# All 31 taps of the first block's depthwise convolution as matmuls with diagonal matrices read from memory

## The chip, the cores and the metric

The kernel runs on 1 core of one Trainium2 chip, in one launch. The metric is device time in microseconds (us) of that core; the figure for a kernel is the median of its runs. Before the change it is 2170.08 us, the median of 3 runs from 2164.84 to 2173.29 us.

## The reference

The program is a network of two blocks over 256 tokens of width 1024. The first block has two layers (`DEPTH = 2`), and each of them has a mixer with three branches: a gated delta rule, a convolution branch and a softmax attention with a forgetting gate ("fox"). What the change touches is the convolution branch:

```python
CONV_WIDTH = D_MODEL // 4      # 256 channels
CONV_KERNEL = 31

def causal_depthwise_conv(x, w):
    k_width, channels = w.shape
    return lax.conv_general_dilated(
        x, w[:, None, :], window_strides=(1,), padding=[(k_width - 1, 0)],
        dimension_numbers=('NWC', 'WIO', 'NWC'), feature_group_count=channels)

# in hybrid_mixer, once a layer
glu_a, glu_b = jnp.split(c_glu, 2, axis=-1)
u = glu_a * jax.nn.sigmoid(glu_b)
u = causal_depthwise_conv(u, cnv_dw_w) + cnv_dw_b
o_b = jax.nn.silu(layer_norm(u, cnv_ln_g, cnv_ln_b))
...
mixed = jnp.concatenate([o_a, o_b, o_c], axis=-1) * mix_scale
return jnp.einsum('bte,ed->btd', mixed, w_out)
```

Each channel has its own 31 taps; output t of a channel is the sum over j of `w[j] * u[t - 30 + j]`. All values are float32.

## The kernel before, in words

The stages follow one another: first block, layer 0 (mixer, dense feed-forward), layer 1 (mixer, mixture of experts), then the second block. `mixer1` is called once a layer, with l = 0 and l = 1. Its matrix products are split in three: a float32 weight tile that has landed in `raw` is rounded on ScalarE to `wh` (line 172), the remainder `wl` is made on VectorE (line 174), and three single-pass matmuls (lines 183 to 185) take the place of one float32 product. A product of two plain float32 operands is recorded as two MATMUL instructions, here called two passes.

Weights come by `load` (line 166): one DMA of up to 1 MB issued by SyncE into one of four `raw` buffers, in rotation. A load waits until the four-before-it buffer is free, that is until its `wh` and `wl` have been made.

Inside `mixer1` the generators `inverse`, `scan`, `fox`, `conv` and `gates` are emitted one after another. A scheduler then orders each engine's instructions by a simulated timeline in which what was emitted earlier goes first when it is ready. So the matmuls of `conv` and, behind them, of `gates` (`proj_b`, 48 matmuls) are put where the delta rule's inverse and scan and the attention leave TensorE free. Each engine then works through its list strictly in that order.

`conv` (lines 739 to 785) works on tiles with the 128 channels of a half on the partitions and 256 tokens along the free dimension. `cup` holds the gated input behind 30 zeros, so tap j of half c reads `up[:, c, j:j + T]`. The last taps of each half (6 in layer 0, 8 in layer 1) are matmuls: ScalarE scales the identity by the tap's column into `dgt` (line 756, two buffers), and a float32 matmul adds into the PSUM tile `a_conv` (recorded at line 362, the helper `mm`). The other taps (25 or 23 a half) are a chain on VectorE into `ccv`: line 762 for the first, line 764 for the rest. Line 765 adds the two parts. What follows in `conv` is the layer norm over channels with two sums on TensorE (`f_cmean`, `f_cvar`), the sigmoid, and the product.

At the end of the mixer the convolution's two halves become chunks 3 and 4 of the transposed operand `xT` (lines 802 and 803), the attention's chunks 5 to 7 and the delta rule's, behind the gates, 0 to 2 (`split_t`, lines 267, 277, 278). Then four `proj_b` products with `w_out` follow, each of which goes through the chunks in the order 0 to 7.

The names in the rows: `a_pB` is a `proj_b` product, `f_fl` are the attention's logits, `g_S`, `g_o` and `g_ws` belong to the scan, `g_lb`, `g_x` and `g_u` to the inverse. Instructions from `mm` all carry line 362.

Of the kernel before, what the change touches and what calls it, by code (L numbers as in the profile page):

```python
# [9 lines left out]
F32 = mybir.dt.float32  # L10
# [4 lines left out]
AF = mybir.ActivationFunctionType  # L15
ALU = mybir.AluOpType
# [4 lines left out]
P = 128  # L21
D = 1024
KC = D // P
T = 256
# [12 lines left out]
def make_consts():  # L37
    i = np.arange(P)
    r, c = i[:, None], i[None, :]
    same = (r // 64) == (c // 64)  # L40
    out = {}
    out["ident"] = (r == c)
    out["anti"] = (r + c == P - 1)
    out["tri"] = (r <= c)
    out["tri64"] = (r <= c) & same
    out["one64"] = same
    out["strict"] = (r < c)
    out["mcaus"] = np.where(c <= r, 0.0, NEG)
    out["iota"] = np.broadcast_to(c, (P, P))
    out["one16"] = (r // 16) == (c // 16)  # L50
    out["id64"] = (r % 64 == c[:, :64])
    out["mcaus64"] = np.where(r % 64 <= c[:, :64], 0.0, NEG)
    out["mstrict64"] = np.where(r % 64 < c[:, :64], 0.0, NEG)
    out["low32"] = (r % 32 == c[:, :32]) | ((r % 32 >= 16) & (c[:, :32] < 16))
    out["id16"] = (r % 16 == c[:, :16])
    out["in16"] = (r // 16 % 4 == c[:, :4])
    out["even16"] = (r // 16 % 2 == c[:, :2])
    out["even32"] = (r // 32 % 2 == c[:, :2])
    return np.ascontiguousarray(np.concatenate([np.asarray(out[n]).astype(np.float32) for n, _ in CONSTS], 1))
# [22 lines left out]

PCOLS1 = []
for _l in range(2):
    PCOLS1 += [(f"rowp{_l}", 24), (f"cw{_l}", 36), (f"mix{_l}", 8), (f"gnw{_l}", 1), (f"dww{_l}", 62), (f"dwb{_l}", 2),
               (f"clg{_l}", 2), (f"clb{_l}", 2)]
PCOLS1 += [("mix0g", 8), ("mix0b", 8)]
PCOLS2 = [("f1n", 8), ("mxn", 8), ("f2n", 8), ("men", 8), ("aqg", 1), ("akg", 1), ("mqg", 1), ("mkg", 1),
# [15 lines left out]
class Net:  # L104
# [249 lines left out]
    def mixer1(self, l, x, xT):  # L354
        nc, A, ident = self.nc, self.A, self.ident
        V, S, PE = nc.vector, nc.scalar, nc.tensor
        wA, wB, wS = A["w_in_a"], A["w_in_b"], A["w_in_s"]
        mp = self.mp
        half = (slice(0, 64), slice(64, 128))

        def mm(out, lhsT, rhs, start=True, stop=True, **kw):
            PE.matmul(out, lhsT, rhs, start=bool(start), stop=bool(stop), skip_group_check=True, **kw)


        rowp = self.col1(f"rowp{l}")
# [53 lines left out]
        cw = self.col1(f"cw{l}")  # L419
# [192 lines left out]
        def spare(c):  # L612

            names = TILES_A[2 * c:2 * c + 2]
            ps = self.proj_a(wA[l, c][:, :1024 * len(names)], xT, tiles=len(names))
            for i, n in enumerate(names):
                if n[0] == "v":
                    value(ps[:, i, :], int(n[1]))
                else:
                    S.activation({"b": glu[:, 0:2], "a": glu[:, 2:4], "f": foxqk[:, 0:3], "g": foxqk[:, 3:6]}[n[0]][:, int(n[1]), :],  # L620
                                 ps[:, i, :], AF.Copy)
# [116 lines left out]
        cv, csq = mp.tile([P, 2, T], F32, name="ccv"), glu[:, 0:2, :]  # L738

        def conv():  # L740

            for c in GLUC:
                spare(c)
            sg = glu[:, 0:2, :]
            self.sigmoid(sg, sg)
            up = mp.tile([P, 2, 30 + T], F32, name="cup")
            V.memset(up[:, :, 0:30], 0.0)
            V.tensor_tensor(up[:, :, 30:], glu[:, 2:4, :], sg, op=ALU.mult)
            yield
            near = 31 - (6, 8)[l]  # L750
            dw, db = self.col1(f"dww{l}"), self.col1(f"dwb{l}")
            pc = self.ps("a", "conv").rearrange("p (c n) -> p c n", c=2)
            for c in range(2):
                for j in range(near, 31):
                    dg = mp.tile([P, P], F32, name="dgt", bufs=2)
                    S.activation(dg, ident, AF.Copy, scale=dw[:, c * 31 + j:c * 31 + j + 1])
                    mm(pc[:, c, :], dg, up[:, c, j:j + T], start=j == near, stop=j == 30)
            for c in range(2):
                for j in range(near):
                    w = dw[:, c * 31 + j:c * 31 + j + 1]  # L760
                    if j == 0:
                        V.tensor_scalar(cv[:, c, :], up[:, c, 0:T], w, db[:, c:c + 1], op0=ALU.mult, op1=ALU.add)
                    else:
                        V.scalar_tensor_tensor(cv[:, c, :], up[:, c, j:j + T], w, cv[:, c, :], op0=ALU.mult, op1=ALU.add)
            V.tensor_tensor(cv, cv, pc, op=ALU.add)
            yield
            ps = self.ps("f", "cmean")
            for c in range(2):
                mm(ps[:, :T], self.ones, cv[:, c, :], start=c == 0, stop=c == 1)
            for c in range(2):  # L770
                V.scalar_tensor_tensor(cv[:, c, :], ps[:, :T], -1.0 / 256, cv[:, c, :], op0=ALU.mult, op1=ALU.add)
            S.activation(csq, cv, AF.Square)
            ps = self.ps("f", "cvar")
            for c in range(2):
                mm(ps[:, :T], self.ones, csq[:, c, :], start=c == 0, stop=c == 1)
            crs = glu[:, 2, :]
            self.rsqrt(crs, ps[:, :T], 1.0 / 256, 1e-5)
            lg_, lb_ = self.col1(f"clg{l}"), self.col1(f"clb{l}")
            for c in range(2):
                V.tensor_tensor(cv[:, c, :], cv[:, c, :], crs, op=ALU.mult)  # L780
                V.tensor_scalar(cv[:, c, :], cv[:, c, :], lg_[:, c:c + 1], lb_[:, c:c + 1], op0=ALU.mult, op1=ALU.add)
            V.tensor_scalar(csq, cv, -40.0, None, op0=ALU.max)
            self.sigmoid(csq, csq)
            V.tensor_tensor(cv, cv, csq, op=ALU.mult)
            yield
# [14 lines left out]
        for c in range(2):  # L800
# [3 lines left out]
                                   op0=ALU.mult, op1=ALU.subtract)  # L804
# [949 lines left out]
def pack_b(w, cols=256):  # L1754

    s, n, c = w.shape[:-2], len(w.shape) - 2, w.shape[-1]
    k = w.shape[-2] // P
    w = w.reshape(s + (k, P, c // cols, cols))
    w = w.transpose(tuple(range(n)) + (n + 2, n + 1, n, n + 3))
    return np.ascontiguousarray(w).reshape(s + (c // cols, P, k * cols))  # L1760
# [10 lines left out]
def chan(v, n):  # L1771

    return v.reshape(n, P).T
# [8 lines left out]
def zeros(*s):  # L1782
    return np.zeros(s, np.float32)


def pack_first(I):
    out = {"consts": make_consts()}
    w = I["w_in"]
    a = np.concatenate([w[:, :, W_IN_A], zeros(2, D, 128)], 2)
    out["w_in_a"] = pack_a(a)  # L1790
    out["w_in_b"] = pack_b(w[:, :, W_IN_B])
    out["w_in_s"] = pack_b(w[:, :, W_IN_S], 18)[:, 0]
    out["w_out"] = pack_b(I["w_out"])
    cols = {}
    for l in range(2):
        cw = I["gdn_conv_w"][l]
        cw = np.concatenate([cw[:, 384:768], cw[:, 0:384], cw[:, 768:]], 1)
        rowp = np.concatenate([I["gdn_dt_bias"][l], zeros(6), I["fox_f_bias"][l], I["gdn_a_log"][l]])
        cols[f"rowp{l}"] = np.broadcast_to(rowp, (P, 24))
        cols[f"cw{l}"] = cw.reshape(4, 9, P).transpose(2, 1, 0).reshape(P, 36)  # L1800
        cols[f"mix{l}"] = chan(I["mix_scale"][l], 8)
        cols[f"gnw{l}"] = np.concatenate([I["gdn_norm_w"][l]] * 2)[:, None]
        cols[f"dww{l}"] = I["cnv_dw_w"][l].reshape(31, 2, P).transpose(2, 1, 0).reshape(P, 62)
        cols[f"dwb{l}"] = chan(I["cnv_dw_b"][l], 2)
        cols[f"clg{l}"] = chan(I["cnv_ln_g"][l], 2)
        cols[f"clb{l}"] = chan(I["cnv_ln_b"][l], 2)
    cols["mix0g"], cols["mix0b"] = chan(I["ln_mix_g"][0], 8), chan(I["ln_mix_b"][0], 8)
    out["pcol1"] = np.ascontiguousarray(np.concatenate([cols[n] for n, _ in PCOLS1], 1))
    out["ln_mix"] = np.concatenate([np.stack([I["ln_mix_g"][l], I["ln_mix_b"][l]]) for l in range(2)])
    out["ln_ffn"] = np.concatenate([np.stack([I["ln_ffn_g"][l], I["ln_ffn_b"][l]]) for l in range(2)])  # L1810
    out["ffn_w1"] = pack_a(I["ffn_w1"][0])
    out["ffn_w3"] = pack_a(I["ffn_w3"][0])
    out["ffn_w2"] = pack_rows(I["ffn_w2"][0])
    out["router"] = pack_b(I["moe_router"][0], NE)[0]
    for n in ("moe_w1", "moe_w3"):
        w = I[n][0].reshape(NE, 2, 4, P, 7, 512).transpose(0, 4, 1, 3, 2, 5)
        out[n] = np.ascontiguousarray(w).reshape(NE, 7, 2, P, 2048)
    out["moe_w2"] = pack_rows(I["moe_w2"][0])
    return out
# [94 lines left out]
```

## Time and profile before

| | |
|---|---|
| time, median of 3 runs | 2170.08 us |
| the profiled execution's own time | 2177.81 us |
| its span | 2176.0 us |
| TensorE (PE) busy | 2079.3 us, 96% |
| VectorE (DVE) busy | 1295.8 us, 60% |
| ScalarE (ACT) busy | 1017.1 us, 47% |
| mixer of layer 0, its end (output projection) | about 181 us into the span |
| mixer of layer 1, its end (output projection) | about 586 us into the span |
| read from memory | 536.72 MB |

Times inside the span are counted from its start. PEclk is the TensorE clock that was granted, as a share of full speed: 1.00 is 2.4 GHz and 0.50 is 1.2 GHz. A matmul's recorded duration holds its latency in the pipeline, so the distance from one start to the next is what an instruction costs in a run of them; "busy" counts overlapping durations once. An engine works through its instructions in order, so what stands behind a waiting instruction waits too.

### The profile page before, as it was taken

The page shows a single profiled execution, that of the slowest core. Times are in us where ns is not written, and L with a number is a line of the kernel's source. Part 1 is how long each engine was busy: PE and PEld are TensorE (multiplying, and loading weights), DVE is VectorE, ACT ScalarE, POOL GpSimd, SP SyncE. Part 2 cuts the span into 40 slices and gives each one's busy share as a digit, 9 for nine tenths or more (in the row PEclk, how much of TensorE's full clock was granted, in tenths as well). Part 3 has the DMA queues.
Part 4 walks back from the last instruction along what each step waited for, and adds up shares of the span by engine and source line. Part 5 has one row for each costly group of instructions (what it writes and reads, how often), then busy time and mean ns, then how long its engine had stood idle before and what let it go on. Part 6 is the DMA issues. An engine that isn't in the chain of part 4 may idle for free. (4 is left out here: it accounts for less than half of the span.)

```text
span 2176.0 us, 31850 instructions
## 1 busy us (share of the span) xinstructions
PE 2079.3 (96%) x12770; PEld 1598.7 (73%) x12770; DVE 1295.8 (60%) x1903; ACT 1017.1 (47%) x1445; POOL 12.7 (1%) x27
## 2 busy tenths in 40 slices
PE   8998999899979999999999999999899999999998
PEld 7887999778766565565565565555699988888997
DVE  6767955676666555454564465454555568765444
ACT  6545444464435454444454454443444444644443
POOL 0000000000000000000000000000000000000000
PEclk9979999998889999999999999999999999999999
DMA  6313675422359999999999999999455553444552
GB/s 236 104 44 118 213 258 182 137 90 96 139 178 347 364 406 378 415 415 371 401 372 383 400 389 393 421 417 398 168 192 180 190 183 126 136 164 155 186 183 98
DMA packets 78987, 545.36 MB, mean 251 GB/s; under 512 B 8960, under 2 KB 11272, under 8 KB 13936
## 3 DMA queue, kind: packets, MB, share of 16 engines
q1 hardware_dynamic: 76112, 527.40, 63.8%
q0 software_dynamic: 2720, 15.84, 2.0%
q8 instruction: 103, 1.69, 0.3%
q14 instruction: 52, 0.43, 0.1%
HBM read 536.72 MB, written 6.49 MB: 250 GB/s over the span
## 5 line engine op out<-in xcount | busy, mean ns | idle before, releaser
L174 DVE TENSOR_TENSOR wl<-raw,wh 128x1024 fp32r<-128x1024 f32 (+1 forms) x662 | 798.1, 1217 | 432.3 <-ACT wh L172 420.5
L172 ACT ACTIVATE wh<-raw 128x1024 fp32r<-128x1024 f32 (+1 forms) x662 | 690.7, 1054 | 627.9 <-PE a_pA L184 270.3
L183 PE MATMUL a_pA<-xTh,wh 128*128 128x256 f32 x1456 | 419.0, 289 | 6.2 <-ACT foxqk L620 3.5
L185 PE MATMUL a_pA<-xTh,wl 128*128 128x256 f32 x1456 | 415.5, 286 | 0.8 <-DVE wl L174 0.7
L184 PE MATMUL a_pA<-xTl,wh 128*128 128x256 f32 x1456 | 415.6, 286 | 0.4 <-DVE xTl L278 0.2
L183 PEld LDWEIGHTS a_pA<-xTh,wh 128*128 128x128 f32 x1456 | 280.8, 193 | 14.7 <-ACT foxqk L620 5.6
L184 PEld LDWEIGHTS a_pA<-xTl,wh 128*128 128x128 f32 x1456 | 281.0, 193 | 5.3 <-issue 3.2
L185 PEld LDWEIGHTS a_pA<-xTh,wl 128*128 128x128 f32 x1456 | 280.8, 193 | 3.8 <-issue 2.2
L1033 PE MATMUL a_up<-raw,xef 128*64 128x512 f32 x896 | 213.5, 596 | 0.0
L184 PE MATMUL a_up<-wl,xeh 128*128 128x512 f32 x448 | 180.7, 403 | 0.5 <-DVE wl L174 0.4
L183 PE MATMUL a_up<-wh,xeh 128*128 128x512 f32 x448 | 177.7, 400 | 0.0
L185 PE MATMUL a_up<-wh,xel 128*128 128x512 f32 x448 | 177.3, 396 | 0.0
L1033 PEld LDWEIGHTS a_up<-raw,xef 128*64 128x64 f32 x896 | 65.1, 137 | 127.8 <-issue 122.3
L1038 DVE TENSOR_TENSOR mos<-mos,a_up 128x512 f32<-128x512 f32 x42 | 28.8, 685 | 200.3 <-PE a_up L1033 149.8
L183 PE MATMUL a_pB<-wh,xTh 128*128 128x256 f32 x480 | 141.5, 296 | 5.7 <-ACT glu L620 3.2
L185 PE MATMUL a_pB<-wh,xTl 128*128 128x256 f32 x480 | 138.6, 291 | 1.6 <-DVE xTl L278 1.6
L184 PE MATMUL a_pB<-wl,xTh 128*128 128x256 f32 x480 | 139.8, 292 | 0.0
L1066 PE MATMUL y_y<-raw,mof 128*64 128x512 f32 x448 | 132.8, 602 | 0.7 <-ACT mof L1052 0.7
L184 PEld LDWEIGHTS a_up<-wl,xeh 128*128 128x128 f32 x448 | 84.6, 189 | 34.5 <-issue 11.4
L183 PEld LDWEIGHTS a_up<-wh,xeh 128*128 128x128 f32 x448 | 84.7, 189 | 28.1 <-ACT wh L172 7.3
L185 PE MATMUL acc_acc<-wh,ffl 128*128 128x512 f32 x264 | 102.0, 392 | 0.0
L184 PE MATMUL acc_acc<-wl,ffh 128*128 128x512 f32 x264 | 101.9, 392 | 0.0
(556 smaller groups left out, 2703.2 us busy)
## 6 DMA issues: line engine op xcount, KB each, us to landing
raw<-in_moe_w_dram SPq DMA_DIRECT2D x336, 1024.0 KB, 9.2
raw<-in_ffn_in_dram SPq DMA_DIRECT2D x44, 1024.0 KB, 4.9
raw<-in_ffn_w_dram SPq DMA_DIRECT2D x33, 1024.0 KB, 5.0
raw<-in_w_in_a_dram SPq DMA_DIRECT2D x24, 1024.0 KB, 4.9
raw<-in_ffn_out_dram SPq DMA_DIRECT2D x22, 1024.0 KB, 4.9
raw<-in_w_out_dram SPq DMA_DIRECT2D x12, 1024.0 KB, 4.9
raw<-in_w_in_g_dram SPq DMA_DIRECT2D x12, 1024.0 KB, 4.9
raw<-in_w_in_b_dram SPq DMA_DIRECT2D x6, 1024.0 KB, 5.1
```

The source lines that it names most:

```text
L172: nc.scalar.activation(wh[:, :m], raw[:, o:o + m], AF.Copy)
L174: nc.vector.tensor_tensor(wl[:, :m], raw[:, o:o + m], wh[:, :m].bitcast(F32), op=ALU.subtract)
L183: mm(out, lh, rh, start=start, stop=False, skip_group_check=True)
L184: mm(out, lh, rl, start=False, stop=False, skip_group_check=True)
L185: mm(out, ll, rh, start=False, stop=stop, skip_group_check=True)
L1033: PE.matmul(ps[r], xe[0][:, k0, r], w[:, k * 512:k * 512 + 512], start=k0 == 0, stop=k0 == 7, skip_group_check=True)
L1038: V.tensor_tensor(s, s, pp[1], op=ALU.mult)
L1066: PE.matmul(py[h][r], hf[:, k, r], w[:, j * 1024 + h * 512:j * 1024 + h * 512 + 512], start=b == 0 and k == 0, stop=b == 6 and k == 3, ski ...
```

## The change

In both mixers all 62 products of a half and a tap become float32 matmuls. The diagonal matrices are no longer made on ScalarE: the host lays them out as an input `w_tap` (2 layers, 4 pieces, 128 x 2048; 1 MB a piece, 16 matrices a piece, 14 in the last), and `conv` reads the four pieces with `load`, by SyncE into the `raw` buffers, and uses them as they land, without `wh` and `wl`. The VectorE chain and the addition of the two parts are gone; instead two ACTIVATE instructions bring the PSUM tile to `ccv` and add the bias. The loads stand, in order of emission, between those for the gated input and the one for the gates.

```diff
-    PCOLS1 += [(f"rowp{_l}", 24), (f"cw{_l}", 36), (f"mix{_l}", 8), (f"gnw{_l}", 1), (f"dww{_l}", 62), (f"dwb{_l}", 2),
+    PCOLS1 += [(f"rowp{_l}", 24), (f"cw{_l}", 36), (f"mix{_l}", 8), (f"gnw{_l}", 1), (f"dwb{_l}", 2),
...
-            near = 31 - (6, 8)[l]
-            dw, db = self.col1(f"dww{l}"), self.col1(f"dwb{l}")
+            db = self.col1(f"dwb{l}")
             pc = self.ps("a", "conv").rearrange("p (c n) -> p c n", c=2)
+            for i in range(4):
+                raw = self.load(A["w_tap"][l, i]).rearrange("p (j n) -> p j n", n=P)
+                for n in range(16 * i, min(16 * i + 16, 62)):
+                    c, j = n // 31, n % 31
+                    mm(pc[:, c, :], raw[:, n % 16, :], up[:, c, j:j + T], start=n == 0, stop=n == 61)
             for c in range(2):
-                for j in range(near, 31):
-                    dg = mp.tile([P, P], F32, name="dgt", bufs=2)
-                    S.activation(dg, ident, AF.Copy, scale=dw[:, c * 31 + j:c * 31 + j + 1])
-                    mm(pc[:, c, :], dg, up[:, c, j:j + T], start=j == near, stop=j == 30)
-            for c in range(2):
-                for j in range(near):
-                    w = dw[:, c * 31 + j:c * 31 + j + 1]
-                    if j == 0:
-                        V.tensor_scalar(cv[:, c, :], up[:, c, 0:T], w, db[:, c:c + 1], op0=ALU.mult, op1=ALU.add)
-                    else:
-                        V.scalar_tensor_tensor(cv[:, c, :], up[:, c, j:j + T], w, cv[:, c, :], op0=ALU.mult, op1=ALU.add)
-            V.tensor_tensor(cv, cv, pc, op=ALU.add)
+                S.activation(cv[:, c, :], pc[:, c, :], AF.Identity, bias=db[:, c:c + 1])
...
+    taps = zeros(2, 64, P, P)
+    i = np.arange(P)
+    taps[:, :62, i, i] = I["cnv_dw_w"].reshape(2, 31, 2, P).transpose(0, 2, 1, 3).reshape(2, 62, P)
+    out["w_tap"] = np.ascontiguousarray(taps.reshape(2, 4, 16, P, P).transpose(0, 1, 3, 2, 4)).reshape(2, 4, P, 2048)
...
-        cols[f"dww{l}"] = I["cnv_dw_w"][l].reshape(31, 2, P).transpose(2, 1, 0).reshape(P, 62)
```

## Rows read from the trace of the kernel before

**Rows 1.** The page: busy time of each engine; granted clock in 40 slices.
```profile
PE 2079.3 (96%) x12770; PEld 1598.7 (73%) x12770; DVE 1295.8 (60%) x1903; ACT 1017.1 (47%) x1445; POOL 12.7 (1%) x27
...
PEclk9979999998889999999999999999999999999999
```
**Rows 2.** Windows, stretches of both mixers: length, busy per engine (instructions), clock, DMA.
```profile
core 0: us, PE busy (x) PEld busy (x) DVE busy (x) ACT busy (x) POOL busy (x), PEclk, DMA share, GB/s
...
122.20:146.10 23.90, 23.90 (x191) 16.58 (x187) 12.90 (x38) 8.85 (x32) 0.00 (x0) 0.50 0.01 2
146.10:165.80 19.70, 18.84 (x185) 16.94 (x183) 16.50 (x38) 9.15 (x18) 0.00 (x0) 1.00 0.16 54
165.80:181.00 15.20, 10.82 (x64) 8.85 (x65) 11.48 (x26) 9.70 (x23) 2.06 (x4) 0.86 0.31 118
...
525.00:552.30 27.30, 27.30 (x210) 19.18 (x210) 14.01 (x41) 10.36 (x36) 0.00 (x0) 0.50 0.00 1
552.30:573.10 20.80, 20.80 (x191) 18.36 (x190) 15.38 (x33) 9.99 (x19) 0.00 (x0) 1.00 0.02 4
573.10:586.00 12.90, 8.03 (x52) 5.86 (x51) 9.52 (x23) 8.92 (x21) 0.53 (x1) 1.00 0.96 384
```
**Rows 3.** Timeline of VectorE in mixer 0, an idle time in the half-clock stretch.
```profile
129.31 0.69 DVE L661 TENSOR_REDUCE fsx<-f_fl 128x2 f32<-128x512 f32 x1 [4.07 <-PE f_fl L362]
```
**Rows 4.** Timeline of TensorE, the mixers' ends, with the idle time before.
```profile
165.83 1.13 PE L362 MATMUL f_cmean<-ccv,ones 128*128 128x256 f32 x4 [0.81 <-DVE ccv L765]
...
174.49 0.66 PE L267 MATMUL g_tr<-call,mixed 128*128 128x128 f32 x4 [1.39 <-DVE mixed L816]
175.88 0.39 PE L183 MATMUL a_pB<-wh,xTh 128*128 128x256 f32 x1 [0.73 <-ACT xTh L277]
...
585.98 0.38 PE L183 MATMUL a_pB<-wh,xTh 128*128 128x256 f32 x1 [1.35 <-ACT xTh L802]
```
**Rows 5.** Tile ccv: the chain on VectorE and the addition of its end.
```profile
L764 DVE SCALAR_TENSOR_TENSOR ccv<-cup,p,ccv x92: 443/477/486, 122.6 to 565.4; 128x256 f32<-128x256 f32 x92
...
L765 DVE TENSOR_TENSOR ccv<-ccv,a_conv x2: 673/681/689, 165.1 to 571.7; 128x512 f32<-128x512 f32 x2
```
**Rows 6.** Tile dgt: duration in ns, min/median/max, first and last start, forms.
```profile
L362 PE MATMUL a_conv<-cup,dgt x56: 377/483/795, 123.0 to 571.3; 128*128 128x256 f32 x56
L756 ACT ACTIVATE dgt<-call,p x28: 385/401/404, 17.5 to 569.6; 128x128 f32<-128x128 f32 x28
```
**Rows 7.** Timeline of TensorE in mixer 0: start us, us, instruction, count.
```profile
77.67 1.88 PE L362 MATMUL g_lb<-sg,call 128*128 128x512 f32 x4
...
123.01 2.08 PE L362 MATMUL a_conv<-cup,dgt 128*128 128x256 f32 x4
125.02 0.79 PE L362 MATMUL f_fl<-rowsT,unit_m 18*128 18x256 f32 x2
...
156.74 1.08 PE L362 MATMUL a_conv<-cup,dgt 128*128 128x256 f32 x4
157.75 0.56 PE L362 MATMUL g_S<-late,kd 64*64 64x64 f32 x12
```
**Rows 8.** Groups by line and form: busy us, mean ns of one, idle before.
```profile
L362 PE MATMUL g_lb<-sg,call 128*128 128x512 f32 x24 | 11.8, 591 | 0.0
```
**Rows 9.** Windows of tile dgt alone: length, PE, PEld, ACT, clock, DMA.
```profile
122.20:146.10 23.90, 6.59 (x12) 3.35 (x12) 2.32 (x6) 0.50 0.01 2
```
**Rows 10.** Windows of tile a_pB alone: length, PE, PEld, DVE, ACT, clock, DMA.
```profile
146.10:165.80 19.70, 6.32 (x42) 5.49 (x42) 0.00 (x0) 0.60 (x1) 1.00 0.16 54
```
**Rows 11.** Timeline of SyncE's issues in mixer 0; DMA issue of one weight, KB, us to landing.
```profile
85.13 0.33 SPq L166 DMA_DIRECT2D raw<-in_w_in_b_dram  x1
93.27 19.83 SPq L166 DMA_DIRECT2D raw<-in_w_out_dram  x4
156.09 73.92 SPq L166 DMA_DIRECT2D raw<-in_ffn_w_dram  x8
...
raw<-in_w_out_dram SPq DMA_DIRECT2D x12, 1024.0 KB, 4.9
```

## The prediction

> **What bounds the kernel now.** I read the page first, for the engine that fills the span: TensorE is busy for 96% of it, and the row of the granted clock, at 9 (full) nearly everywhere, dips to 8 in slices that hold the mixers of layer 0 and layer 1 [rows 1]. Then I cut the stretches of both mixers in which the convolution runs into windows, by the granted clock [rows 2]. The reader is to see three stages in each. First a stage of 23.90 us (27.30 us in layer 1) in which TensorE is busy throughout and yet has half its clock, 0.50. Then one of 19.70 us (20.80 us) at full clock with TensorE busy for 18.84 us (all 20.80 us). Last a tail of 15.20 us (12.90 us) in which TensorE is busy for only 10.82 us (8.03 us), because the layer norm of the convolution, the gates and the transposes hand work to and fro.
>
> So up to the tail TensorE sets the pace. The timeline of VectorE bears it out from the other side: that engine, which carries the chain of taps, sits idle for 4.07 us before an instruction that waits for the attention's logits [rows 3], with taps queued behind it. The chain of taps shows on the path in one place only: TensorE waits 0.81 us for the addition at its end in mixer 0 [rows 4]. In the tail the waits are for the gated delta rule's result (1.39 us), for its transposes (0.73 us), and in layer 1 for the convolution's chunk of the output projection (1.35 us) [rows 4].
>
> **What the change removes.** On VectorE 92 chain instructions at 0.477 us and the four first ones, of another form, counted alike: 46 us in both mixers; and two additions of 0.68 us [rows 5]. On ScalarE 28 scaled identities at 0.40 us, 11 us [rows 6]. Both engines have free time in every stage (VectorE is busy for 12.90 of 23.90 and 16.50 of 19.70 us) [rows 2], so of this only what lies in the tail counts: the wait of 0.81 us, and little else. I book it with the tail below.
>
> **What it adds on TensorE.** Before, 56 passes in all [rows 6], which are 24 in mixer 0 (6 taps of 2 halves, 2 passes each) and 32 in mixer 1. After, 62 matmuls a mixer, 124 passes each: 100 more in mixer 0, 92 more in mixer 1, 192 in all. The price of one at full clock lies between two rows. A run of four passes took 1.01 us from its start to the start of the next group, 0.25 us each, with the first weight load not hidden [rows 7]. A longer stream is cheaper: four float32 passes of 512 columns took 1.88 us [rows 7], one of them has a recorded duration of 0.591 us [rows 8], so three distances fill the other 1.29 us, 0.43 us each; half of that, 0.215 us, for 256 columns. The new passes need nothing but `cup` and a landed piece, so they come in long runs, and I take 0.215 us: 192 x 0.215 = 41.3 us. At 0.25 us it would be 48 us. At half clock four passes took 2.01 us, 0.50 us each in a short run [rows 7]; in a long one it would be twice 0.215, 0.43 us.
>
> **Where these passes go.** In order of emission they stand behind the inverse, the scan and the attention, and ahead of the gates. So they take the gaps that those leave. In the half-clock stage the gaps are small: 12 of the 24 passes were run there in mixer 0, 6.59 of 23.90 us [rows 9], and the rest of the stage belongs to the attention's logits, on 18 rows of the array in the row shown [rows 7], and the inverse. A few gate matmuls in these gaps are replaced by passes. I take ten more passes there in both mixers together, at 0.215 us extra each: 2 us; between 0 and 20 us, if up to half of the added passes fell there. All others pile up after it. The full-clock stage was full already; there 42 gate matmuls, 6.32 us, were part of the filling [rows 10], and now they come after the convolution's. The stage grows by what is added, nearly one for one.
>
> **The tail.** Here something comes back. The gates' projection, about 6 us of dense work, now comes behind the convolution's last pass, and so covers part of the convolution's layer norm. The idle time of TensorE in the two tails is 15.20 - 10.82 = 4.4 us and 12.90 - 8.03 = 4.9 us [rows 2]. I take both back, 9.3 us; the other bound is nothing, as the gates' own sigmoid and products then come last and leave a tail of their own.
>
> **The clock.** In the half-clock stages TensorE was busy without a pause, and the clock stayed at 0.50 (1.2 GHz) for 23.90 and 27.30 us [rows 2]. The Trainium skill (TensorE: Matmul & The Clock Gate, "Why this matters for your kernels") says to keep TensorE busy continuously to get past the gate to the full clock. By that rule these stages should have been at full clock, and the trace disagrees. So I don't count on added busy time alone to lift it. For a lift speaks that the added passes use all 128 rows; against it, how few of them find room before 146 us. In the forecast both stages stay at half clock.
>
> **Loads, copies and the constants.** Four loads of 1 MB a mixer are added on SyncE's queue, ahead of the gates' load and the four of `w_out`. Those went out at 85.13 us and between 93.27 and about 113 us [rows 11]. These are the moments when buffers come free, and the first four now belong to the pieces. A load of this size lands in 4.9 us [rows 11], so the pieces are there by about 118 us, before the first pass at 123.01 us [rows 7]: nothing lost. The DMA engines are nearly idle then (share 0.01) [rows 2]. What is behind them moves late: the gates' load waits for the 16 matmuls of the first piece, the first three of `w_out` for the other pieces, the fourth for the gates' split. The third of them waits for the convolution's last pass; but it is needed only after the gates, the tail and two output products, so I cost it at nothing. With that cover gone it costs a landing and a split, an estimated 4.9 + 2 us a mixer. The next stage's first load, at 156.09 us before [rows 11], slips too; the output projection hides it. The bias is added by four ACTIVATEs of two halves of 256 columns, nearest to the scaled identity of 128 columns at 0.40 us [rows 6], in place of the two additions of 0.68 us [rows 5]: between 0 and 1 us lost, I take nothing. The table of constants loses 124 of its 290 columns; it is loaded behind others at the start, where the kernel waits for the inputs: nothing, at most 1 us gained.
>
> **Sum.** 41.3 + 2 - 9.3 = 34 us. The profiled execution took 2177.81 us around its span of 2176.0, 7.7 us more than the median of the runs, 2170.08; the difference carries over, so I add it to the median: 2204 us.
>
> **Rivals.**
> 1. *The clock comes back.* The place is the half-clock stages. If the full-row passes come in long unbroken runs early in them, they run at 2.4 GHz and give back up to half their length, 12.0 + 13.7 = 25.6 us. Then 34 - 2 - 25.6 = +6 us: 2176, no change that can be measured; if each stage recovers only in its middle, about +20, 2190. It decides from whether such runs stand before 130 us. For it: a pass is 128 rows deep. Against it: the convolution had half its passes in that stage before, and the clock did not rise. If, beyond that, VectorE's freed queue shortens the chains of attention and scan, the end comes slightly faster than before. The skill's rule named above would make this rival the outcome.
> 2. *Late weights.* The four loads behind the pieces arrive when TensorE already needs them: +7 us a mixer on the forecast, 2218. For it: four buffers hold raw pieces until TensorE, not a split, has read them. Against it: the DMA engines have room [rows 2].
> 3. *The passes themselves run at half clock.* If a stream of them doesn't lift the clock, 192 x 0.43 = 82.6 us less the tail's 9.3: +73, 2243. Against it: passes ran at 1.00 after 146.1 us, among others [rows 2, 7].
>
> **How the numbers follow.** Chances: forecast 0.55, clock back 0.25, late weights 0.12, half clock 0.08. What a measurement of this kernel can tell from no change is about 0.5%, 11 us: 2159 to 2181 us. Rival 1 spreads over faster (0.05), same (0.12) and slower (0.08); the rest is slower: 0.83. The forecast's own range is 2190 to 2218. The whole range goes down to rival 1's sum of 2176, and up to 2236, between late weights and half clock.
>
> **What would show it.** In the trace of the changed kernel: 248 passes on `a_conv`, with starts 0.215 us apart in long runs; the first stage of each mixer still at 0.50 for over 20 us; the stage behind it 18 to 20 us longer, full of `a_conv`, with the gates' projection at its end; less idle TensorE time in the tails; no wait of `a_conv` or of the output projection for a DMA. A clock at 1.00 from about 130 us on makes the forecast wrong on the low side; waits for `raw`, or `a_conv` passes of 0.43 us after 150 us, on the high side.

## The result, and the profile after

The changed kernel took 2221.98 us (median of 4 runs, 2216.98 to 2230.57) against 2169.47 us of the kernel before (4 runs): a ratio of 1.0247 [1.0205, 1.0289], slower, and 18 us more than the 2204 us forecast. The profiled execution of the changed kernel was the fastest of its four (2216.98 us, span 2215.2), the one of before (2177.81) longer than all four of its kernel, so the two traces differ by 39 us where the medians differ by 52.5.

The page: TensorE's busy row, and its granted clock in 40 slices [rows 1].

```profile
PE 2107.2 (95%) x12962; PEld 1627.5 (73%) x12962; DVE 1259.2 (57%) x1805; ACT 1007.6 (45%) x1421; POOL 12.7 (1%) x27
...
PEclk9998999998888999999999999999999999999999
```

VectorE is relieved of 37 us and ScalarE of 10, and the span grows. To see where, I cut one window a mixer, from the start of `cup` to the end of the last addition behind the output projection. (In the kernel before that is 203.73 and 609.33 us; the 181 and 586 us given further up as the mixers' ends lie within the output projection.) In the kernel before (length, busy time per engine, clock, DMA share, GB/s):

```profile
119.42:203.73 84.31, 78.35 (x624) 65.82 (x623) 59.24 (x133) 38.53 (x86) 2.06 (x4) 0.82 0.22 78
522.25:609.33 87.08, 81.43 (x633) 67.48 (x633) 52.48 (x118) 35.30 (x82) 0.53 (x1) 0.82 0.32 121
```

In the changed one, the same two windows, and below them the stages within them [rows 2]:

```profile
119.49:218.69 99.20, 87.70 (x714) 76.32 (x713) 43.33 (x84) 37.32 (x78) 2.07 (x4) 0.95 0.35 119
542.81:652.62 109.81, 98.40 (x710) 84.20 (x706) 38.05 (x73) 33.86 (x72) 0.53 (x1) 0.84 0.40 143
...
119.49:146.00 26.51, 26.51 (x293) 20.70 (x293) 7.32 (x22) 8.73 (x30) 0.00 (x0) 1.00 0.08 24
146.00:172.93 26.93, 26.93 (x167) 22.80 (x165) 6.90 (x11) 4.51 (x6) 0.00 (x0) 1.00 0.40 134
172.93:185.90 12.97, 8.33 (x62) 7.60 (x61) 5.77 (x12) 8.12 (x14) 0.00 (x0) 1.00 0.47 162
185.90:196.10 10.20, 4.06 (x18) 3.57 (x19) 7.95 (x19) 5.38 (x14) 2.07 (x4) 0.50 0.23 75
...
542.81:568.20 25.39, 25.39 (x198) 18.52 (x194) 5.45 (x15) 6.53 (x25) 0.00 (x0) 0.50 0.00 1
568.20:607.24 39.04, 39.04 (x256) 33.22 (x256) 8.85 (x17) 6.54 (x11) 0.00 (x0) 1.00 0.32 108
```

Each window splits into three: idle time of TensorE (length less busy), what the clock cost (an estimate: half of the busy time in stretches at 0.50), and the rest, its work at full clock. Worked out so for mixer 0 / mixer 1, in us, with the kernels of the experiments below:

| kernel | length | idle | clock | work |
|---|---|---|---|---|
| before | 84.3 / 87.1 | 6.0 / 5.7 | 15.1 / 15.4 | 63.2 / 66.1 |
| changed | 99.2 / 109.8 | 11.5 / 11.4 | 2.0 / 14.4 | 85.7 / 84.0 |
| gates first | 105.8 / 106.0 | 7.5 / 7.5 | 12.4 / 12.6 | 85.9 / 85.8 |
| gates between | 103.0 / 105.8 | 7.5 / 7.5 | 8.6 / 10.9 | 87.0 / 87.4 |
| half the passes | 95.0 / 94.2 | 11.4 / 11.5 | 12.6 / 11.7 | 70.9 / 71.0 |
| half the rows | 106.4 / 112.3 | 11.5 / 11.4 | 9.2 / 16.0 | 85.7 / 84.9 |
| none on TensorE | 81.1 / 78.9 | 8.8 / 7.9 | 15.5 / 13.8 | 56.8 / 57.2 |

With the gates moved (gates first, gates between), `cup` itself starts 4.7 us earlier in mixer 0, at 114.8 us, so those windows are longer by that at their front.

From before to changed: work +40.4, idle +11.3, clock -14.1, together +37.6 of the 39 us; outside the windows 5.6 us are added between the mixers and 4.1 us go behind them. The added work is that of the passes, here the `a_conv` rows of the changed kernel by their tile [rows 6]:

```profile
L362 PE MATMUL a_conv<-cup,raw x248: 377/378/742, 123.7 to 606.9; 128*128 128x256 f32 x124
```

The idle time has one main place. TensorE's timeline, with a long run of passes and the wait in front of the delta rule's transposes (`g_tr`) in each mixer; the bracket holds the idle time and what ended it [rows 4]:

```profile
164.28 5.02 PE L362 MATMUL a_conv<-cup,raw 128*128 128x256 f32 x22
...
191.69 1.51 PE L267 MATMUL g_tr<-call,mixed 128*128 128x128 f32 x6 [8.99 <-DVE mixed L809]
...
625.90 1.59 PE L267 MATMUL g_tr<-call,mixed 128*128 128x128 f32 x6 [8.91 <-DVE mixed L809]
```

Both mixers have a wait of 9 us there, where rows 4 had 1.39 us. What leads up to it stands in the timelines of ScalarE and VectorE:

```profile
179.56 0.60 ACT L783 ACTIVATE gate<-a_pB 128x512 f32<-128x512 f32 x1 [1.20 <-PE a_pB L185]
181.00 0.83 ACT L299 ACTIVATE late<-gate 128x768 f32<-128x768 f32 x1
182.45 0.94 ACT L300 ACTIVATE late<-late,bias 128x768 f32<-128x768 f32 x1
184.29 0.86 ACT L301 ACTIVATE late<-late 128x768 f32<-128x768 f32 x1
...
190.64 0.91 ACT L795 ACTIVATE xTh<-ccv,msc 128x256 fp32r<-128x256 f32 x2 [0.66 <-DVE ccv L777]
```

```profile
185.83 0.95 DVE L785 TENSOR_TENSOR gate<-gate,late 128x768 f32<-128x768 f32 x1
...
190.99 1.02 DVE L809 TENSOR_TENSOR mixed<-late,mixed 128x384 f32<-128x384 f32 x2
```

The gates' projection ends with the copy at 179.56, and copy, sigmoid, product and norm take 12 us until `mixed` is there at 192. Before, the copy stood at 162.30 us, and most of this lay beside the scan:

```profile
162.30 0.60 ACT L790 ACTIVATE gate<-a_pB 128x512 f32<-128x512 f32 x1 [2.76 <-PE a_pB L185]
```

The convolution's own layer norm, which starts from the last pass at 173 us, has its result (`xTh` from `ccv`) at 191.6 us, at nearly the same moment. So two chains end there, and both stand behind the last pass.

The loads are harmless [rows 11]; SyncE's issues of the changed kernel:

```profile
84.27 20.35 SPq L166 DMA_DIRECT2D raw<-in_w_tap_dram  x4
...
151.28 22.01 SPq L166 DMA_DIRECT2D raw<-in_w_out_dram  x4
```

The pieces are issued by 105 us, before the first pass at 123.7, and no wait of TensorE in the two windows is for a DMA.

### The profile page after: what moved, and what is told of

Its sections match the earlier page's. It is cut to its first block, busy times and chain, and to the rows that moved or that the text cites. A ratio compares the mean times of both kernels' runs of the same rounds, so it can differ in the third digit from the quotient of the medians.

```text
span 2215.2 us, 32125 instructions
## 1 busy us (share of the span) xinstructions
PE 2107.2 (95%) x12962; PEld 1627.5 (73%) x12962; DVE 1259.2 (57%) x1805; ACT 1007.6 (45%) x1421; POOL 12.7 (1%) x27
## 5 line engine op out<-in xcount | busy, mean ns | idle before, releaser
L184 PEld LDWEIGHTS a_up<-wl,xeh 128*128 128x128 f32 x448 | 84.6, 189 | 34.8 <-issue 11.4
```

The source lines that it names most:

```text
L184: mm(out, lh, rl, start=False, stop=False, skip_group_check=True)
```

## The experiments

The theory: passes are paid on TensorE's path, and the 9 us come from the gates' projection being queued behind the last pass. Rivals: late loads, the half-clock stage, or simply a bad order of the gates. All runs were timed beside the kernel before, in three groups: 2173.65 us (17 runs) with gates first, one piece, the source of the matrices and half the passes; 2173.58 (23) with gates between, the same move in the kernel before, no tap on TensorE and the second look; 2173.53 (11) with three taps, half the rows and taps first. The changed kernel was timed before these, beside the 2169.47 us above, so the ratios with their intervals compare kernels more safely than the medians do.

**Gates first.** In the changed kernel:

```diff
-        self.emit(inverse(), scan(), fox(), conv(), gates())
+        taps = conv()
+        self.emit(inverse(), scan(), fox())
+        next(taps)
+        self.emit(gates(), taps)
```

> The changed kernel with the gates' projection emitted ahead of the convolution's passes (after its gated input). Theory, the gates end the mixer: in the changed kernel TensorE idles 8.99 us in mixer 0 before the delta rule's transposes, because the gates' projection, and with it its sigmoid, comes behind the last pass. With the gates first that idle time goes, the convolution's layer norm then ends the mixer, 4 to 9 us a mixer come back: 2204 to 2214 us. Rival, the last pass ends the mixer either way (it comes about 6 us later and its layer norm takes 15 us): 2218 to 2226 us, and a like idle time in front of the output projection's chunk 3.

Measured: 2212.87 us, ratio 1.0197 [1.0171, 1.0224], against 1.0247 [1.0205, 1.0289]: 9 us less in the medians, with intervals that overlap. The profiled executions, both at a mean clock of 0.973, are 5.1 us apart. In TensorE's timeline the wait of `g_tr` is gone, and a shorter one follows, for the convolution's layer norm:

```profile
183.88 0.82 PE L267 MATMUL g_tr<-call,mixed 128*128 128x128 f32 x6
...
196.81 0.58 PE L183 MATMUL a_pB<-wh,xTh 128*128 128x256 f32 x1 [6.42 <-ACT xTh L798]
```

Idle falls by 4 us a mixer. But the passes now start only at 153 us, and the clock changed with them: over the whole span idle time falls by 8.0 us and the clock takes 3.9 us more.

**Gates between.** Gates emitted between the second and the third piece, so that passes start early again:

```diff
+                if i == 2:
+                    yield
                 raw = self.load(A["w_tap"][l, i])...
```

> The changed kernel with the gates' projection emitted between the second and the third piece of taps. Theory (the tail): 60 of the 124 passes then stand behind the gates' projection and cover its sigmoid, products, norm and transposes, so the 9 us wait of g_tr is gone; the convolution's layer norm ends the mixer as with the gates first: 2208 to 2216 us, 6 to 12 us less than the changed kernel. Rival (the clock): gates first won because its passes all ran after the half-clock stage and the gates' matmuls inside it; here passes start at 123 us again, so that gain goes and the time is the changed kernel's, 2218 to 2224 us.

Measured: 2209.68 us, 1.0164 [1.0143, 1.0184]: 12 us below the changed kernel in the medians, with intervals apart, and the best of those with all taps on TensorE. The profiled executions are 7.3 us apart, and over the whole span 8.6 us of idle time are gone, with the clock's cost within 1 us of the changed kernel's. Idle is 7.5 us a mixer as with the gates first, with the same last wait of 6.42 us for the convolution's layer norm. So the passes behind the gates' projection hide its tail; that they left the early stage was not needed. What they don't hide is the other chain, the layer norm behind the last pass.

**The same move in the kernel before.** The diff of "Gates first", applied to the kernel before.

> The kernel before, with the gates' projection emitted ahead of the convolution's taps instead of behind them (the control to the same move in the changed kernel, which gave about 9 us back). Theory: the order costs time only where 124 passes stand ahead of the gates; the kernel before has 24 and 32 passes there, which TensorE runs in gaps, and g_tr waited 2.3 us in its first tail, not 9. So 2162 to 2180 us, ratio 0.997 to 1.003. Rival: gates behind the convolution is a bad order in any kernel, then 5 to 9 us less than before (ratio 0.996 to 0.997 or lower) and a better kernel.

Measured: 2180.04 us, 1.0027 [1.0015, 1.0040], some 6 us more. Gates behind the convolution are not a bad order in itself: with 24 and 32 passes it is the better one, and here too the wait moves to the convolution's layer norm (5.21 us). It becomes bad with 124 passes ahead of the gates.

**One piece.** The four pieces' loads are replaced by one a mixer, used four times:

```diff
-            for i in range(4):
-                raw = self.load(A["w_tap"][l, i])...
+            raw = self.load(A["w_tap"][l, 0])...
+            for i in range(4):
```

> The changed kernel with one piece of diagonal matrices loaded a mixer and used for all 62 products (the output is not the reference's: taps 16 to 61 use the matrices of others); three loads a mixer fewer, and the gates' weights and w_out are fetched early again. Theory, TensorE's order and not the loads: no change, 2216 to 2228 us. Rival, late weights: 7 us a mixer come back, 2208 us or less, and waits for raw go away.

Measured: 2219.23 us, 1.0219 [1.0192, 1.0247], the changed kernel's time within its interval, with the same 9.0 us wait of `g_tr`. Three loads fewer give nothing back: rival 2 falls.

**The source of the matrices alone.** The kernel before with its own 6 and 8 taps a half, their matrices loaded in one piece instead of made by ScalarE:

```diff
+            raw = self.load(A["w_tap"][l])...
...
-                    dg = mp.tile([P, P], F32, name="dgt", bufs=2)
-                    S.activation(dg, ident, AF.Copy, scale=dw[...])
-                    mm(pc[:, c, :], dg, up[:, c, j:j + T], ...)
+                    mm(pc[:, c, :], raw[:, 8 * c + j - near, :], up[:, c, j:j + T], ...)
```

> The kernel before with its own split of taps (6 and 8 a half as matmuls, the others on VectorE), but the 12 and 16 diagonal matrices read from memory in one 1 MB piece a mixer instead of made on ScalarE: one load a mixer more, 28 ScalarE instructions less. Theory, the added matmuls and not the source of the matrices cost the time: as the kernel before, 2160 to 2175 us. Rival, the piece in the ring of raw buffers delays the gates and w_out: 2177 us or more.

Measured: 2172.82 us, 0.9986 [0.9964, 1.0008]: no difference that can be told. With as many taps on TensorE as before, it costs nothing to read the matrices from memory; what costs is the number of taps there.

**Half the passes.** The changed kernel with 124 of its 248 passes:

```diff
-                for n in range(16 * i, min(16 * i + 16, 62)):
+                for n in range(16 * i, min(16 * i + 16, 62), 2):
```

> The changed kernel with every second of the 62 products left out in both mixers (the output is not the reference's), all loads kept: 124 passes fewer. Theory, the passes lie on the path at 0.215 us each: 27 us less than the changed kernel, 2195 us. Rival, part of the cost is a tail that follows the last pass and stays: the same 27 us. Rival, passes hidden in gaps: less than 15 us. Rival, passes mostly at half clock: 40 to 53 us less.

Measured: 2193.75 us, 1.0096 [1.0070, 1.0122], 28 us less than the changed kernel in the medians. By the table the work falls by 14.8 + 13.0 = 27.8 us, 0.224 us a pass. The profiled executions differ by only 21.1 us, as the clock took 8.6 us more over the whole span of this one; so the work of a pass is on the path, and that the medians agree with it to a microsecond is in part chance. The tail stays, though there are half as many passes:

```profile
186.74 1.55 PE L267 MATMUL g_tr<-call,mixed 128*128 128x128 f32 x6 [10.36 <-DVE mixed L809]
```

With 68 passes more than before the kernel is 20 us slower, where 68 x 0.215 is 14.6, and idle time in the two windows is 11.3 us above the kernel before's as with all passes; the tail is a price by itself, not a part of the pass price.

The clock of this run matters below. Mixer 0 fell to 0.50 at 123.61 us, in the middle of its first six passes, which are 128 rows deep and start at 123.27 us:

```profile
123.61:144.10 20.49, 20.49 (x132) 13.92 (x130) 3.58 (x13) 5.54 (x21) 0.00 (x0) 0.50 0.01 2
```

Up to the sixth pass TensorE's list of matmuls is the same, in the same order, as in the changed kernel, which runs these six from 123.65 us on and stayed at 1.00.

**No tap on TensorE.** In the kernel before:

```diff
-            near = 31 - (6, 8)[l]
+            near = 31
```

with the loop over `near..30` and the addition of `pc` gone.

> The kernel before with all 31 taps on VectorE and none on TensorE: 56 passes fewer, 28 chain instructions of 0.477 us more. Theory: every pass on TensorE in these stages is on the path at 0.215 us, downwards as upwards, and VectorE has the room: 12 us less, about 2161 us (ratio 0.9945). Rival: in the tail VectorE's chain is what ends last; it gets 5.7 us longer in mixer 0 and 7.6 us in mixer 1, and the wait for it grows by about as much as TensorE saves: no change or up to 8 us more (ratio 1.000 to 1.004), with the wait of the convolution's mean for its sums at 5 us or more in both mixers.

Measured: 2168.64 us, 0.9980 [0.9964, 0.9997]: 5 us less, and of all the one version whose interval lies below both kernels. The two windows are 11.4 us shorter, near the price of 12: work -15.4, idle +5.1, clock -1.2. The idle time is at the wait of `g_tr` for the norm's products on VectorE:

```profile
170.20 0.66 PE L267 MATMUL g_tr<-call,mixed 128*128 128x128 f32 x2 [4.80 <-DVE mixed L809]
```

Outside the windows 7 us are given back, 5.7 of them between the mixers, where half-clock stretches grew from 13.6 to 27.3 us in sum. So the pass price holds in the mixers, and the rival by half: a wait grew, but at `g_tr`; the convolution's mean waits only 0.38 us for its sums.

**Three taps on TensorE.** `near = 31 - (3, 3)[l]` in the kernel before.

> The kernel before with 3 taps of each half on TensorE in both mixers (24 passes in all, not 56) and 28 on VectorE. By the pass price alone, 32 passes at 0.215 us less: 7 us less. With none on TensorE 12 us were to go and 5 went, as the longer chain on VectorE made the gates' result late. Theory: between the two, 2 to 6 us less than before (ratio 0.997 to 0.999), the chain still near the end of the tail. Rival: the chain is covered again at this split, and it is the full 7 us or more (ratio 0.9965 or lower), better than none on TensorE.

Measured: 2186.60 us, 1.0063 [1.0039, 1.0087]: 13 us slower than before, against both expectations. The windows of `ccv` alone (VectorE's column is the one with the taps), first of this kernel, then with none on TensorE:

```profile
119.00:146.00 27.00, 0.00 (x0) 0.00 (x0) 11.79 (x28) 0.00 (x0) 0.56 0.01 2
```

```profile
119.00:146.00 27.00, 0.00 (x0) 0.00 (x0) 18.59 (x45) 0.00 (x0) 0.62 0.01 2
```

Up to 146 us VectorE does 28 of these here, and 45 with no tap on TensorE. The chain then ends at 172.3 us, not at 156, taking turns with the products of the gates and the norm, and idle time is 13.1 and 12.1 us a mixer. VectorE had time for more (3.08 us idle before 142.78): the order on its queue is a different one. Why it came out so is open; a time between two splits can't be read off a line between them.

**The clock: a second look, and half the rows.** The changed kernel was profiled again, in one run.

> The changed kernel unchanged, a second profile of it. The question is whether the granted clock in the convolution's stage belongs to the kernel or to the execution. In its first profile mixer 0 had no half-clock stage there and mixer 1 had one of 27.3 us. If it belongs to the kernel, the same stretches come again within a microsecond or two. If to the execution, they come elsewhere or with other lengths, and a span that differs by up to half of their difference in length.

Measured: 2218.04 us. Mixer 0 again had no half-clock stretch beside the convolution, and mixer 1 had 30.7 us of it, as at first (23.9 + 6.8 against 3.4 + 27.3). Then the passes were cut to 64 of the 128 rows:

```diff
-mm(pc[:, c, :], raw[:, n % 16, :], up[:, c, j:j + T], ...)
+mm(pc[:, c, :], raw[0:64, n % 16, :], up[0:64, c, j:j + T], ...)
```

> The changed kernel with each of the convolution's products over the first 64 of its 128 rows (part of the convolution is left out); as many passes, of as many columns, in the same order. Theory: TensorE's time for a pass goes by its columns, and the full clock in mixer 0's stage was given for passes over all rows; with half the rows the half-clock stage of 20 to 27 us returns in mixer 0, and the time is up to 12 us more than the changed kernel's: 2225 to 2234 us. Rival: the depth plays no part: mixer 0 stays at 1.00 and the time is the changed kernel's, 2218 to 2224 us.

Measured: 2241.51 us (2229.61 to 2248.15), 1.0316 [1.0283, 1.0349], 20 us more than the changed kernel, above what either account gave. The passes by their tile, and windows of two stretches:

```profile
L362 PE MATMUL a_conv<-cup,raw x248: 373/375/789, 122.0 to 618.8; 64*128 64x256 f32 x124
```

```profile
123.50:137.20 13.70, 13.70 (x115) 9.62 (x114) 1.02 (x3) 3.88 (x16) 0.00 (x0) 0.50 0.00 0
...
539.90:580.90 41.00, 41.00 (x322) 31.51 (x321) 7.46 (x22) 10.40 (x38) 0.00 (x0) 0.50 0.01 1
```

The passes last as long (375 ns against 378), idle and work are within 1 us of the changed kernel's in each mixer, and what differs is the clock: a half-clock stretch of 13.7 us is back in mixer 0, and the one of mixer 1 grew from 27.3 to 41.0 us. Over all executions the mean clock was 0.959 to 0.967 in the six of this run, and 0.966 to 0.973 in the five of the changed kernel. So this kernel got less clock. That the rows of the passes were what kept mixer 0 at 1.00 is not shown: the half-passes run had 20.5 us at 0.50 there, and the one-piece run 17.1 us (122.04 to 139.11), both with passes over all 128 rows. Nor did the rows change alone: behind the first twelve passes the scheduler made runs of 2, 6 and 6 of them where the changed kernel has 6, 12 and 2.

**Taps first.** The changed kernel with the passes emitted ahead of the inverse, the scan and the attention:

```diff
+        attn, taps = fox(), conv()
+        for _ in FOXC:
+            next(attn)
+        next(taps)
+        next(taps)
-        self.emit(inverse(), scan(), fox(), conv(), gates())
+        self.emit(inverse(), scan(), attn, taps, gates())
```

> The changed kernel with the convolution's passes (and the projections that feed the attention) emitted ahead of the inverse, the scan and the attention. The passes then stand in one block of some 27 us right behind cup, where the half-clock stage began. Theory: a dense block of passes over all 128 rows runs at full clock (0.215 us each), so the stretch behind cup reads 1.00; but the inverse and the scan start that much later, with nothing left to fill their gaps, and the half-clock stage comes behind the block: 2222 to 2250 us, not faster than the changed kernel. Rival: the clock, once up, stays up through the inverse and the attention: 10 us or more less than the changed kernel, about 2205 us.

Measured: 2231.62 us, 1.0269 [1.0242, 1.0296]. The block, and the windows of mixer 0 behind it and of mixer 1 behind its own:

```profile
102.81 27.00 PE L362 MATMUL a_conv<-cup,raw 128*128 128x256 f32 x124
```

```profile
102.81:130.00 27.19, 27.19 (x157) 23.57 (x158) 5.34 (x11) 4.73 (x12) 0.00 (x0) 1.00 0.42 155
135.20:165.90 30.70, 29.33 (x253) 25.74 (x253) 3.10 (x4) 7.76 (x22) 0.00 (x0) 0.50 0.10 36
...
572.80:619.80 47.00, 47.00 (x698) 40.50 (x698) 19.34 (x42) 20.97 (x52) 0.00 (x0) 1.00 0.21 70
```

The block runs at 1.00, 0.218 us a pass. Behind it mixer 0 fell to 0.50 for 30.7 us, and mixer 1 did not fall: each account is right in one mixer. It is not faster than the changed kernel; whether it is slower the overlapping intervals leave open. The profiled execution is 15.9 us longer than the changed kernel's, of which 14.1 us are the clock's over the whole span; idle time is the same within 0.4 us, so the later start of inverse and scan did not show as idle time.

## Why the prediction was right in direction and short by 18 us

*The passes.* 192 x 0.215 = 41.3 us, on the path nearly one for one: the work rose by 40.4 us, and half the passes gave back 0.224 us each. In mixer 1 the full-clock stage grew by 18.2 us, to 39.04, as forecast. Right. (The 0.25 us of the four-pass run was not the price of a weight load: the group behind it waited 0.33 us for VectorE's `mixed`.) The 2 us booked for ten more passes at half clock were not due: 8 of the 248 passes ran at 0.50, against 26 of 56 before.

*The tail.* This is the step that failed: "I take both back, 9.3 us". Idle time rose by 11.3 us instead, a miss of 20.6. The gates' projection does cover part of the convolution's layer norm, as it said, but about 6.5 us of 18.6: that norm's `xTh` comes at 191.6 us, 18.6 us after the last pass. And the other bound, which I named and put at nothing, was too mild: "the gates' own sigmoid and products then come last and leave a tail of their own" has a price of its own, since the 12 us from copy to `mixed` had lain beside the scan and found no work on TensorE to lie beside any more. Measured, the term is +11.3: waits of 9.0 and 8.9 us came, and of the 11.6 us of idle time before 5.0 are left. The gates moved ahead of half the passes took 8.6 us of idle time back, and 7.3 us of time in the profiled executions (12 in the medians); the 6.42 us wait for the layer norm that is left in each mixer is the other chain's share.

*The clock.* "In the forecast both stages stay at half clock." In the profiled execution mixer 1 stayed (25.39 us at 0.50), mixer 0 did not: its 53.4 us from `cup` to the last pass ran at 1.00, and its window lost 13.1 us less than before. So rival 1's outcome came in one mixer of two, but not by its condition: before 130 us there were two runs of six passes, 1.51 us each, no long ones, and the half-passes run, with the same matmuls up to the sixth pass, fell to 0.50 there. What it gave as its reason, "a pass is 128 rows deep", can't be the whole of it either, as those passes were. Which execution gets the full clock in mixer 0 is thus not settled by what TensorE had been given up to that point, and the forecast had no term for it. The sign "a clock at 1.00 from about 130 us on" came, and the time still missed on the high side, as the tail took the gain.

That the sum of this trace comes out near the forecast (+37.6 in the windows and 39 over all, against 34) is luck: the misses of 20.6 us in the tail and 16 us in the clock's terms nearly cancel. The other 13.3 us of the miss are not in the traces at all. They are the distance of the profiled executions from the medians, 8.3 us in the kernel before and 5.0 in the changed one. Two of the changed kernel's four executions, 2225.87 and 2230.57 us, had a mean clock of 0.968 and 0.966, against 0.973 in the other two; over the span 0.007 is about 16 us. They left no trace, so where they lost it, be it in mixer 0's stage, is not shown. And the kernel before, timed again beside the experiments, came to 2173.5 to 2173.7 us in 11 to 23 runs each; against that the change costs 48 us and not 52.

The Trainium skill (TensorE: Matmul & The Clock Gate, "Why this matters for your kernels") asks for continuous work. The 30.7 us of the taps-first run at 0.50, with TensorE busy for 29.33 of them, disagree once more. What decides the level is open.

*Loads, copies, constants.* Costed at nothing, and nothing: no wait for a piece, one piece a mixer takes as long, and matrices from memory cost the kernel before nothing either. Rival 2 falls. Rival 3 falls too: 240 of the 248 passes ran at full clock (52 passes of mixer 1 in 11.50 us, 0.22 each).

## What to carry to other kernels

Where one engine fills the span, work moved to it costs its full duration, however idle the other engine becomes; and what was emitted behind the moved work is late by all of it. Look for the chain that starts behind the new work and has nothing left to lie beside: here it cost a quarter of what the passes did, and a place between two pieces of the new work took most of that back. Split a window into idle time, clock loss and work before trusting a sum that comes out right, and before giving a reason for a clock look in every other trace for a case with the same reason and another clock.

## What was not expected of the hardware

The same matmuls in the same order were granted different clocks: up to the sixth pass of mixer 0 TensorE's list is the same in the changed kernel and in the half-passes run, and the clock stayed at 1.00 in the one (twice, in two profiled executions) and fell to 0.50 for 20.5 us in the other.

Passes over 64 rows, of the same duration (375 ns against 378), came with a lower clock than passes over 128: a mean of 0.959 to 0.967 against 0.966 to 0.973, and 20 us in the median. Their order changed as well, so how much of it is the rows' is open.
